# Attention values by pairs of heads in two column halves of the array, and every sixth unit's exponentials transposed on TensorE

## The chip, the core and the metric

The kernel runs on one core of one Trainium2 chip. The metric is the device time of one execution in microseconds (us). Five engines work side by side and meet at semaphores: TensorE (PE in the rows, its weight loads PEld), VectorE (DVE), ScalarE (ACT), GpSimd (POOL) and SyncE (SP), which issues the DMAs.

## The reference

Two layers of a backbone over 1024 latent tokens and 256 context tokens of width 1024, batch 1. Each layer normalises, projects once into three groups of heads (softmax attention, a bidirectional mLSTM, a pooling mixer), joins the three, projects out, adds to the stream, and then runs a SwiGLU block. The change touches the attention group alone, with 8 query heads of 64 over 2 key and value heads:

```python
s = jnp.einsum('bqhgd,bkhd->bhgqk', qi, k, preferred_element_type=F32) * scale
p = jax.nn.softmax(s, -1).astype(v.dtype)
return jnp.einsum('bhgqk,bkhd->bqhgd', p, v)
```

Latent queries see all 1280 tokens. Context queries see the 256 context tokens, and only in the first layer; the second layer has none.

## The kernel before

Each layer first makes all projections with eight free PSUM banks, and then goes over to a phase "s", in which six banks are two score buffers of three banks (`bank3`, tile `Sp`) and two banks are left for everything else (`bank`, tag `bk`). Operands of most matmuls are split into a high and a low float16 half, and a product is three matmuls (`TERMS`: high by high, high by low, low by high).

The attention loop runs over units. A unit is one head of one block of 128 latent queries; there are 64 in a layer, and layer 0 has four more, each of four heads of one block of context queries. Iteration i of the loop does, in the order of the program:

* `front` of unit i: scores into `Sp` (L1311, six matmuls for 1280 keys), their maximum by DVE (L1315), a small DVE step (L1320), and the exponentials by ACT into `pf` in float32, with their sum into `sums`;
* `split` of unit i-1: the high half `phl` by ACT (by DVE for every eighth unit, L1334), the low half by POOL (L169), and one DMA transpose of both halves into `pT` (L1340, on the queue of SP). There are two buffers of `pf`, three of `phl` and five of `pT`;
* the fill: a step of the output projection (`wout`, L1371, twelve matmuls into a bank `pwo`, which DVE adds to `X`), paced by a budget per iteration;
* `back` of unit i-5: the values. Each 128x128 block of `pT` is the stationary operand, and the 64 columns of V stream past it (L1353), thirty matmuls for a head, into one bank `pv` that is held for all eight heads of a query block.

After the eighth head `att_finish` divides by the sums (`ao`), splits into `aoh` (ACT and DVE) and transposes by DMA into `mixT` (L1365), the operand of the output projection. The framework that builds the kernel lists each engine's instructions by priority and readiness, so that the order on an engine is near the order of the program, but not the same.

Other lines that are used as prices: L919 writes two column halves of a bank with 64-wide stationary operands in the mLSTM part; L618 transposes float32 blocks by TensorE at the end; L471 and L1946 are projections.

Of the kernel before, what the change touches and what calls it, by code (L numbers as in the profile page):

```python
# [9 lines left out]
F32 = mybir.dt.float32  # L10
F16 = mybir.dt.float16
# [7 lines left out]
P = 128  # L19
# [62 lines left out]
def hybrid_kernel(ctx: ExitStack, tc: tile.TileContext, I, out, dbg=None):  # L82
    nc = tc.nc
    V, S, G, TE, DMA = nc.vector, nc.scalar, nc.gpsimd, nc.tensor, nc.sync
    MUL, ADD, SUB, MAX, MIN = ALU.mult, ALU.add, ALU.subtract, ALU.max, ALU.min
# [10 lines left out]
    PFB, PHB, PTB = 2, 3, 5  # L96
# [21 lines left out]
    def bank(name="bk"):  # L118
        return cur["b"].tile([P, 512], F32, tag="bk", name=name)
# [8 lines left out]
    def pt_(shape, dt, tag, bufs=1, name=None):  # L128
        return cur["w"].tile(list(shape), dt, tag=tag, name=name or tag, bufs=bufs)

    def f2k(shape=(P, 512), dt=F32, name="f2k"):
        return pt_(shape, dt, "f2k", F2K[cur["kind"]], name)


    mm = TE.matmul
# [6 lines left out]
    def preload():  # L142

        p = S.preload_act_table_set("natural_log_exp_and_others").ins
        for j in tabs["last"]:
            after(p, j)
        tabs.update(pre=p, last=[], kind="el")

    def act(o, i, f=AF.Copy, **kw):
        if f in (AF.Exp, AF.Ln) and tabs["kind"] != "el":  # L150
            preload()
        b = S.activation(o, i, f, **kw).ins  # L152
        if f in (AF.Exp, AF.Ln):
            after(b, tabs["pre"])
            tabs["last"] = tabs["last"][-7:] + [b]
        elif f in (AF.Tanh, AF.Silu):
            if tabs["kind"] != f:
                for j in tabs["last"]:
                    after(b, j)
                tabs.update(last=[], kind=f)  # L160
            for j in tabs["last"][-1:]:
                after(b, j)
            tabs["last"] = [b]
# [4 lines left out]
    def tt(o, a, b, op, e=None):  # L168
        (e or V).tensor_tensor(o, a, b, op=op)  # L169
# [23 lines left out]
    def pump(n=1):  # L193
        for _ in range(n):
            for g in list(threads):
                try:
                    next(g)
                except StopIteration:
                    threads.remove(g)
# [18 lines left out]
    idn = con.tile([P, P], F32, name="idn")  # L218
# [36 lines left out]
    pv = bank("pv")  # L255
# [203 lines left out]
    TERMS = ((0, 0), (0, 1), (1, 0))  # L459
# [272 lines left out]
    pv = bank("pv")  # L732
# [5 lines left out]
    pv = None  # L738
    nx = {}

    for l in range(DEPTH):
        last = l == DEPTH - 1
        h1 = mixT = h2 = T1
        qkv = actb = T2
# [462 lines left out]
        for (t0, n) in BLOCKS:  # L1207
            if t0 in nx:
                drain(nx.pop(t0))
            for r in range(3):  # L1210
                if t0 >= T and last and r == 2:
                    continue
                if l == 0 and t0 < T:
                    pb = pf0[r][t0 // 512]
                else:
                    pb = bank("pfm")
                    fm(pb[:, :n], wf[r], h1, t0, n)
                held.append((r, t0, n, pb))
                pb = None
# [3 lines left out]
            while held and t0 > 0:  # L1223
                r_, t_, n_, pb = held.pop(0)
                fst[r_](t_, n_, pb[:, :n_])
                pb = None
                pump()
        w = w_get(("in", l, O_MG))
        pb = bank("pmg")
# [66 lines left out]

        class Unit:
            def __init__(self, i, qt, hs, qs):
                self.i, self.qt, self.hs, self.qs = i, qt, hs, qs
                self.nk, self.k0 = (NTOK, 0) if qt < 8 else (TC, T)  # L1300
                self.n = self.nk * len(hs)

# [25 lines left out]
                        accum_out=self.qs[1][:, h:h + 1])  # L1328

            def split(self):  # L1330
                i, n, pf = self.i, self.n, self.pf
                hl = pt_((P, 2, NTOK), F16, "phl", PHB)
                if i % 8 == 0:
                    V.tensor_copy(hl[:, 0, :n], pf[:, :n])  # L1334
                else:
                    act(hl[:, 0, :n], pf[:, :n])
                tt(hl[:, 1, :n], pf[:, :n], hl[:, 0, :n], SUB, G)
                self.pT = pt_((P, 2, 10, P), F16, "pT", PTB)
                if n == NTOK:
                    DMA.dma_start_transpose(out=self.pT.rearrange("p a k c -> p (a k) c"), in_=hl.rearrange("p a t -> p (a t)"))  # L1340
                else:
                    for a in range(2):
                        DMA.dma_start_transpose(out=self.pT[:, a, :n // P], in_=hl[:, a, :n])

            def back(self):
                if self.hs[0] == 0:
                    self.qs[0] = bank("pv")
                nkt = self.nk // P
                for e, h in enumerate(self.hs):
                    kv = h // 4  # L1350
                    for kt in range(nkt):
                        for j, (a, b) in enumerate(TERMS):
                            mm(self.qs[0][:, h * 64:h * 64 + 64], self.pT[:, a, e * nkt + kt],  # L1353
                               qkv[:, 6, b, self.k0 + kt * P:self.k0 + (kt + 1) * P][:, kv * 64:kv * 64 + 64],
                               start=(kt == 0 and j == 0), stop=(kt == nkt - 1 and j == 2))

        def att_finish(qt, pv_, sums):
            V.reciprocal(sums, sums)
            o = f2k((P, 8, 64), F32, "ao")
            tt(o, pv_.rearrange("p (h e) -> p h e", h=8), sums.unsqueeze(2).to_broadcast([P, 8, 64]), MUL)  # L1360
            oh = f2k((P, 4, 2, P), F16, "aoh")
            ov = o.rearrange("p (k x) e -> p k (x e)", x=2)
            act(oh[:, :, 0], ov)
            tt(oh[:, :, 1], ov, oh[:, :, 0], SUB)
            DMA.dma_start_transpose(out=mixT[:, 0:4, :, qt * P:(qt + 1) * P].rearrange("p k a t -> p (k a) t"),  # L1365
                                    in_=oh.rearrange("p k a c -> p (k a c)"))

        def wout(w, k0, m, t0, n, pb):
            for k in range(4):
# [48 lines left out]
        units = []  # L1418
        for qt in range(8):
            qs = [None, pt_((P, 8), F32, "sums", 3)]  # L1420
            units += [Unit(len(units) + h, qt, [h], qs) for h in range(8)]
            if qt < 2 and not last:
                qs = [None, pt_((P, 8), F32, "sums", 3)]
                units += [Unit(len(units) + g, 8 + qt, list(range(4 * g, 4 * g + 4)), qs) for g in range(2)]
        done = [-1]
        nt = {}
        fill = fills()
        nu = len(units)
        budget = 0.0
        fill_ffn = first_ffn()  # L1430

# [4 lines left out]
        for i in range(nu + 5):  # L1436
            now[0] = i
            if i < nu:
                units[i].front()
            if 1 <= i <= nu:  # L1440
                units[i - 1].split()
            if i >= 3:
                budget = min(budget + pace(i / nu), 3.0)
                if budget > 0:
                    c = next(fill, None)
                    if c is None:
                        c = next(fill_ffn, 0)
                    budget -= c
            if i >= 5:
                u = units[i - 5]  # L1450
                u.back()
                if u.hs[-1] == 7:
                    att_finish(u.qt, *u.qs)
                    if u.qt < 8:
                        done[0] = u.qt
                units[i - 5] = u = None
            pump()
        for _ in fill:
            pass
        units = fill = None  # L1460
# [133 lines left out]
        raws, sums, rawuse, made, live_s = {}, {}, {}, {}, [0]  # L1594
# [344 lines left out]
        for bi, (t0, n) in enumerate([(0, 512), (512, 256), (768, 256)] if last else blks):  # L1939
            sums = None if last else Sums(t0, n)  # L1940
            for m in range(NK):
                w = piece("last", m)
                pb = bank("pdn")
# [8 lines left out]
            if bi == 0:  # L1952
# [3 lines left out]
                pb = None  # L1956
# [7 lines left out]
            if bi == 0 and not last:  # L1964
                sums = rms_sum(t0, n)
# [5 lines left out]
            sums = None  # L1971
# [33 lines left out]
```

## Time and profile before

| | us |
|---|---|
| median of three runs | 2797.26 (2795.92 to 2797.89) |
| the profiled execution | 2801.78 |
| its span, first to last instruction | 2800.0 |
| PE busy in the span | 2562.9 (92%) |
| DVE busy | 1883.6 (67%) |
| ACT busy | 1387.2 (50%) |
| POOL busy | 1288.5 (46%) |

A busy time is the time covered by at least one instruction of the engine. Matmuls are pipelined, so that each is shown longer than the distance from one start to the next; distances of starts are read from groups of them. The DMA share is the mean over 16 DMA engines and may go over 1 where packets overlap.

### The profile page before, as it was taken

How to read it: one execution, taken by the hardware profiler on the slowest of the kernel's cores; microseconds unless marked ns; L12 is line 12 of the kernel's file. 1: busy time of each engine (PE TensorE's matmuls, PEld its weight loads, DVE VectorE, ACT ScalarE, POOL GpSimd, SP SyncE). 2: the span in 40 equal slices, each digit the busy share in tenths (PEclk: the TensorE clock that was granted, in tenths of full speed). 3: DMA queues.
4: the chain of work that ended last, by engine and by line, in shares of the span. 5: the costliest groups of instructions: out<-in, count | busy, mean ns of one | idle time of the engine just before them, and what ended most of it. 6: DMA issues, size and time to landing. Idle time of an engine off the chain costs nothing. (4 is left out here: it accounts for less than half of the span.)

```text
span 2800.0 us, 53595 instructions
## 1 busy us (share of the span) xinstructions
PE 2562.9 (92%) x21331; PEld 1496.8 (53%) x21331; DVE 1883.6 (67%) x3217; ACT 1387.2 (50%) x2650; POOL 1288.5 (46%) x979
## 2 busy tenths in 40 slices
PE   7999988887799999999999998988878799999997
PEld 5875555555455555555555674545554344444444
DVE  5458867779856655656566557866677766576666
ACT  5345457776443434434344445466764444444353
POOL 1124446674434434344443213456764555555651
PEclk9999999999899999999999999999999999999999
DMA  9544499996222232322212222499993121211211
GB/s 298 143 122 115 126 208 187 195 186 129 61 83 84 83 88 80 89 84 83 68 39 78 69 61 64 124 183 188 195 188 80 45 61 53 61 53 53 61 53 76
DMA packets 650640, 300.95 MB, mean 107 GB/s; under 512 B 381896, under 2 KB 639764, under 8 KB 649876
## 3 DMA queue, kind: packets, MB, share of 16 engines
q1 hardware_dynamic: 650212, 297.45, 44.2%
q8 instruction: 167, 2.74, 0.4%
q14 instruction: 85, 0.70, 0.1%
q10 hardware_dynamic: 176, 0.07, 0.0%
HBM read 176.19 MB, written 20.87 MB: 70 GB/s over the span
## 5 line engine op out<-in xcount | busy, mean ns | idle before, releaser
L1900 PEld LDWEIGHTS <-hlp 128*128 128x128 f16 x5040 | 492.9, 98 | 610.1 <-issue 49.5
L1900 PE MATMUL Swb<-T,hlp 128*128 128x512 f16 x1920 | 446.4, 382 | 30.8 <-DVE sg L166 14.7
L169 POOL TENSOR_TENSOR phl<-pf,phl 128x1280 f16<-128x1280 f32 (+1 forms) x132 | 346.3, 2625 | 187.7 <-ACT phl L152 129.4
L166 DVE SCALAR_TENSOR_TENSOR hlp<-ws,hlp 128x512 f16<-128x512 f32 (+1 forms) x320 | 228.9, 722 | 150.6 <-ACT hlp L152 119.9
L152 ACT ACTIVATE hlp<-ws 128x512 f16<-128x512 f32 (+1 forms) x320 | 163.6, 518 | 220.1 <-PE Swb L1900 89.8
L152 ACT ACTIVATE pf<-Sp,mx,rq 128x1280 f32<-128x1280 f32 (+1 forms) x144 | 189.2, 1315 | 103.4 <-DVE mx L1320 89.1
L1315 DVE TENSOR_REDUCE mx<-Sp 128x1 f32<-128x1280 f32 (+1 forms) x132 | 194.9, 1477 | 64.5 <-PE Sp L1311 59.5
L1371 PE MATMUL pwo<-T,hl 128*128 128x512 f16 (+1 forms) x960 | 196.5, 356 | 38.0 <-DVE X L166 20.0
L1900 PE MATMUL Swc<-T,hlp 128*128 128x512 f16 x960 | 227.2, 379 | 0.0
L1311 PE MATMUL Sp<-T 128*128 128x512 f16 (+1 forms) x800 | 172.9, 355 | 58.5 <-ACT pf L152 56.1
L1900 PE MATMUL Swb<-tq,hlp 128*128 128x512 f16 x960 | 220.5, 379 | 2.5 <-ACT T L152 2.3
L466 PE MATMUL pfm<-T,hl 128*128 128x512 f16 (+1 forms) x1032 | 217.0, 364 | 4.2 <-ACT E L152 4.1
L152 ACT ACTIVATE T<-sg 128x512 f16<-128x512 f32 (+1 forms) x170 | 100.0, 600 | 229.4 <-POOL sg L169 154.8
L166 DVE SCALAR_TENSOR_TENSOR hlp<-st,hlp 128x256 f16<-128x256 f32 (+1 forms) x201 | 141.6, 709 | 89.8 <-ACT hlp L152 75.1
L169 POOL TENSOR_TENSOR ws<-st 128x256 f32<-128x256 f32 (+1 forms) x97 | 102.2, 1061 | 185.6 <-DMA st<-in_w_ffn_down_dram 83.3
L1912 PE MATMUL dx<-T,hlp 128*128 128x256 f16 x1440 | 177.9, 273 | 10.6 <-DVE hlp L166 6.4
L169 POOL TENSOR_TENSOR X<-X,T 128x512 f32<-128x512 f32 x80 | 113.2, 1415 | 147.4 <-DVE X L166 111.1
L1900 PE MATMUL Swa<-T,hlp 128*128 128x512 f16 x720 | 169.1, 380 | 0.0
L1912 PEld LDWEIGHTS <-hlp 128*128 128x128 f16 x1440 | 139.3, 100 | 43.0 <-issue 9.1
L1371 PEld LDWEIGHTS <-hl 128*128 128x128 f16 x960 | 98.0, 103 | 119.8 <-issue 53.3
L152 ACT ACTIVATE phl<-pf 128x1280 f16<-128x1280 f32 (+1 forms) x115 | 144.9, 1261 | 30.3 <-DMA pT<-phl 27.9
L152 ACT ACTIVATE hlp<-st 128x256 f16<-128x256 f32 (+1 forms) x201 | 101.2, 510 | 114.6 <-PE Swb L1900 73.2
(320 smaller groups left out, 4733.6 us busy)
## 6 DMA issues: line engine op xcount, KB each, us to landing
T<-in_w_ada_dram SPq DMA_DIRECT2D x48, 512.0 KB
rawa<-in_w_ada_dram SPq DMA_DIRECT2D x48, 512.0 KB
st<-in_w_in_dram SPq DMA_DIRECT2D x32, 512.0 KB
st<-in_w_out_dram SPq DMA_DIRECT2D x64, 256.0 KB
st<-in_w_ffn_gate_dram SPq DMA_DIRECT2D x32, 512.0 KB
st<-in_w_ffn_up_dram SPq DMA_DIRECT2D x30, 512.0 KB
st<-in_w_ffn_down_dram SPq DMA_DIRECT2D x30, 512.0 KB
xs<-X SPq DMA_DIRECT2D x4, 2048.0 KB
```

Source lines behind the costliest of these rows:

```text
L152: b = S.activation(o, i, f, **kw).ins
L166: V.scalar_tensor_tensor(o, a, s, b, op0=o0, op1=o1)
L169: (e or V).tensor_tensor(o, a, b, op=op)
L466: mm(o, w[:, a, k, :], h[:, k, b, t0:t0 + n], start=(k == 0 and j == 0), stop=(k == nk - 1 and j == 2))
L1311: mm(Sp[:, e * nk + b0:e * nk + b0 + m], ql, qkv[:, 4 + h // 4, a, k0 + b0:k0 + b0 + m], start=(a == 0), stop=(a == 1), skip_group_check=True)
L1315: r = V.tensor_reduce(mx[:, :ne], Sp[:, :n].rearrange("p (e k) -> p e k", e=ne), axis=AX.X, op=MAX)
L1371: mm(pb, w[:, a, k, :], mixT[:, k0 + k, b, t0:t0 + n], start=(k == 0 and j == 0), stop=(k == 3 and j == 2))
L1900: mm(o, w[:, a, k, :], B[:, b], start=(s in "172" and k == 0 and j == 0), stop=(k == kh(i) - 1 and j == 2), skip_group_check=True)
L1912: mm(dbank[i][:, r * 256:(r + 1) * 256], w[:, a, k, :], B[:, b], start=(first and k == 0 and j == 0), stop=(not first and k == kh(i) - 1 a ...
```

## The change

Units of one head are counted, and the 6th, 12th and so on (ten in each layer) are turned on TensorE: there is no `phl`, no POOL work and no DMA. The unit's ten 128x128 blocks of `pf` are transposed in float32 in groups of four, four and two into a bank `turn`; ACT writes the high half from it into `pT`, and DVE the low half. The three groups stand ahead of the fill, behind it, and behind the values.

The values are made for two heads at a time, every second iteration. Now V is the stationary operand, 64 columns wide, and 128 columns of `pT` stream; the even head writes partitions 0 to 63 of a bank and the odd head 64 to 127, in turn, so that the result comes out already transposed. The reciprocals of the two sums are spread over 64 partitions each by two float32 matmuls against the identity, copied out by ACT, multiplied in by DVE, and ACT and DVE write the two halves straight into `mixT`. The bank is held for one pair. `att_finish` and its DMA transpose go.

```diff
             def split(self):
                 i, n, pf = self.i, self.n, self.pf
+                if i in turned:
+                    self.pT = pt_((P, 2, 10, P), F16, "pT", PTB)
+                    self.parts = [self.turn(k, min(4, 10 - k)) for k in range(0, 10, 4)]
+                    return
...
-            def back(self):
-                if self.hs[0] == 0:
-                    self.qs[0] = bank("pv")
...
-                            mm(self.qs[0][:, h * 64:h * 64 + 64], self.pT[:, a, e * nkt + kt],
-                               qkv[:, 6, b, self.k0 + kt * P:self.k0 + (kt + 1) * P][:, kv * 64:kv * 64 + 64],
-                               start=(kt == 0 and j == 0), stop=(kt == nkt - 1 and j == 2))
-        def att_finish(qt, pv_, sums):
-            V.reciprocal(sums, sums)
-            o = f2k((P, 8, 64), F32, "ao")
-            tt(o, pv_.rearrange("p (h e) -> p h e", h=8), sums.unsqueeze(2).to_broadcast([P, 8, 64]), MUL)
-            oh = f2k((P, 4, 2, P), F16, "aoh")
...
-            act(oh[:, :, 0], ov)
-            tt(oh[:, :, 1], ov, oh[:, :, 0], SUB)
-            DMA.dma_start_transpose(out=mixT[:, 0:4, :, qt * P:(qt + 1) * P].rearrange("p k a t -> p (k a) t"),
-                                    in_=oh.rearrange("p k a c -> p (k a c)"))
+            def turn(self, k, m):
+                def go():
+                    tb = bank("turn")
+                    for c in range(m):
+                        TE.transpose(tb[:, c * P:(c + 1) * P], self.pf[:, (k + c) * P:(k + c + 1) * P], idn)
+                    tv = tb[:, :m * P].rearrange("p (k c) -> p k c", k=m)
+                    act(self.pT[:, 0, k:k + m], tv)
+                    tt(self.pT[:, 1, k:k + m], tv, self.pT[:, 0, k:k + m], SUB)
+                return go
+        def values(us, pair):
...
+            V.reciprocal(sums[:, hs[0]:hs[0] + 2], sums[:, hs[0]:hs[0] + 2])
+            pb = bank("pv")
+            for g, h in enumerate(hs):
+                mm(pb[64 * g:64 * g + 64, P:2 * P], sums[:, h:h + 1].to_broadcast([P, 64]), idn, start=True, stop=True)
+            u = f2k((P, 2, P), F32, "ao")
+            act(u[:, 0], pb[:, P:2 * P])
+            for kt in range(nkt):
+                for j, (a, b) in enumerate(TERMS):
+                    for g, h in enumerate(hs):
+                        un = us[g if len(us) == 2 else 0]
+                        mm(pb[64 * g:64 * g + 64, 0:P], qkv[:, 6, b, k0 + kt * P:k0 + (kt + 1) * P][:, kv * 64:kv * 64 + 64],
+                           un.pT[:, a, un.hs.index(h) * nkt + kt], start=(kt == 0 and j == 0), stop=(kt == nkt - 1 and j == 2),
+                           skip_group_check=True)
+            tt(u[:, 1], pb[:, 0:P], u[:, 0], MUL)
+            q = slice(qt * P, (qt + 1) * P)
+            act(mixT[:, pair, 0, q], u[:, 1])
+            tt(mixT[:, pair, 1, q], u[:, 1], mixT[:, pair, 0, q], SUB)
...
+        turned = [u.i for u in units if len(u.hs) == 1][5::6]
...
+            if parts:
+                parts.pop(0)()
             if i >= 3:
...
+            if parts:
+                parts.pop(0)()
             if i >= 5:
                 u = units[i - 5]
-                u.back()
-                if u.hs[-1] == 7:
-                    att_finish(u.qt, *u.qs)
-                    if u.qt < 8:
-                        done[0] = u.qt
+                if len(u.hs) > 1:
+                    for e in range(0, len(u.hs), 2):
+                        values([u], u.hs[e] // 2)
+                elif u.hs[0] % 2 == 0:
+                    values([u, units[i - 4]], u.hs[0] // 2)
+                if u.hs[-1] in (6, 7) and u.qt < 8:
+                    done[0] = u.qt
                 units[i - 5] = u = None
+            while parts:
+                parts.pop(0)()
```

## Rows read from the trace of the kernel before

**Rows 1.** Windows: stretch, length, busy PE, PEld, DVE, ACT, POOL, clock, DMA share.

```profile
374.00:656.00 282.00, 238.62 (x2845) 155.83 (x2844) 210.60 (x254) 198.91 (x274) 188.46 (x82) 0.94 1.07 194
1827.00:2091.00 264.00, 212.59 (x2564) 134.17 (x2562) 182.16 (x213) 182.71 (x228) 177.13 (x73) 0.95 1.05 190
...
450.00:500.00 50.00, 46.71 (x572) 30.30 (x570) 37.32 (x46) 36.77 (x49) 33.35 (x13) 0.97 1.12 188
```

**Rows 2.** The same windows for the fill's line L1371 alone.

```profile
374.00:656.00 282.00, 107.30 (x553) 56.23 (x554) 0.94 1.07 194
1827.00:2091.00 264.00, 82.31 (x360) 36.95 (x361) 0.95 1.05 190
```

**Rows 3.** Line L1315 in each stretch: count, ns min/median/max, first and last start.

```profile
L1315 DVE TENSOR_REDUCE mx<-Sp x68: 1215/1483/1494, 375.1 to 653.5; 128x1 f32<-128x1280 f32 x64, 128x4 f32<-128x1024 f32 x4
...
L1315 DVE TENSOR_REDUCE mx<-Sp x64: 1474/1483/1493, 1827.4 to 2089.3; 128x1 f32<-128x1280 f32 x64
```

**Rows 4.** Tiles pT and aoh: DMA transposes on the queue of SP.

```profile
L1340 SPq DMA_TRANSPOSE pT<-phl x128: 2977/3284/5487, 383.1 to 2098.1; - x128
...
L1365 SPq DMA_TRANSPOSE T<-aoh x18: 1231/1283/2072, 428.3 to 2111.0; - x18
```

**Rows 5.** Waits, 374 to 656 us: total us, times, longest.

```profile
ACT phl L152 <- DMA pT<-phl: 11.8, 11, 2.3
```

**Rows 6.** Waits, 1827 to 2091 us.

```profile
ACT phl L152 <- DMA pT<-phl: 16.1, 11, 3.2
```

**Rows 7.** Timeline, 564 to 574 us, the end of a query block.

```profile
567.28 0.68 DVE L169 TENSOR_TENSOR ao<-pv,sums 128x512 f32<-128x512 f32 x1
567.89 2.73 DVE L166 SCALAR_TENSOR_TENSOR hl<-st,hl 128x512 f16<-128x512 f32 x1
568.00 0.63 ACT L152 ACTIVATE aoh<-ao 128x512 f16<-128x512 f32 x1 [1.95 <-DVE ao L169]
...
570.53 1.48 DVE L1315 TENSOR_REDUCE mx<-Sp 128x1 f32<-128x1280 f32 x1
571.94 1.02 DVE L169 TENSOR_TENSOR aoh<-ao,aoh 128x512 f16<-128x512 f32 x1
...
573.53 1.03 PE L1371 MATMUL pwo<-T,hl 128*128 128x512 f16 x3 [3.39 <-DVE X L166]
```

**Rows 8.** Timeline of PE at several places (start, length, group); last, line L919's durations.

```profile
548.43 1.04 PE L1353 MATMUL pv<-T,pT 128*128 128x64 f16 x30
549.31 1.25 PE L1311 MATMUL Sp<-T 128*128 128x512 f16 x6
...
151.16 0.39 PE L919 MATMUL pu<-X,kh 128*64 128x65 f16 x12
151.48 2.74 PE L471 MATMUL ptm<-hl,T 128*128 128x128 f16 x46
...
2769.36 1.04 PE L618 MATMUL pout<-idn,X 128*128 128x128 f32 x8
2770.23 0.82 PE L1946 MATMUL pdn<-T,hlp 128*128 128x256 f16 x6
...
L919 PE MATMUL pu<-X,kh x432: 192/195/263, 142.8 to 1671.8; 128*64 128x65 f16 x144
```

**Rows 9.** Lines by form: busy us, mean ns, idle before and its releasers.

```profile
L169 POOL TENSOR_TENSOR phl<-pf,phl 128x1280 f16<-128x1280 f32 x128 | 337.8, 2641 | 183.7 <-ACT phl L152 126.0 <-DVE phl L1334 47.8 <-DMA pT<-phl 3.7
...
L152 ACT ACTIVATE phl<-pf 128x1280 f16<-128x1280 f32 x112 | 141.8, 1267 | 30.2 <-DMA pT<-phl 27.9 <-ACT pf L152 0.5
...
L152 ACT ACTIVATE X<-pf 128x512 f16<-128x512 f32 x6 | 3.4, 587 | 0.2
...
L166 DVE SCALAR_TENSOR_TENSOR X<-pf,X 128x512 f16<-128x512 f32 x6 | 3.8, 677 | 0.0
...
L152 ACT ACTIVATE sa<-pada 128x128 f32<-128x128 f32 x80 | 21.9, 273 | 4.6 <-PE pada L483 3.5
...
L169 DVE TENSOR_TENSOR num<-pxi,tmq 128x130 f32<-128x130 f32 x68 | 17.4, 284 | 7.8 <-PE pxi L998 7.5
```

More of the change, by code (lines that the diff above doesn't have):

```diff
@@ L1298, in __init__ @@
             def __init__(self, i, qt, hs, qs):
-                self.i, self.qt, self.hs, self.qs = i, qt, hs, qs
+                self.i, self.qt, self.hs, self.qs, self.parts = i, qt, hs, qs, []
                 self.nk, self.k0 = (NTOK, 0) if qt < 8 else (TC, T)
@@ L1343, in split @@
                         DMA.dma_start_transpose(out=self.pT[:, a, :n // P], in_=hl[:, a, :n])
-            def back(self):
-                if self.hs[0] == 0:
-                    self.qs[0] = bank("pv")
[L1348 to L1352, printed above, removed]
-                            mm(self.qs[0][:, h * 64:h * 64 + 64], self.pT[:, a, e * nkt + kt],
-                               qkv[:, 6, b, self.k0 + kt * P:self.k0 + (kt + 1) * P][:, kv * 64:kv * 64 + 64],
-                               start=(kt == 0 and j == 0), stop=(kt == nkt - 1 and j == 2))
@@ L1357, in att_finish @@
-        def att_finish(qt, pv_, sums):
-            V.reciprocal(sums, sums)
-            o = f2k((P, 8, 64), F32, "ao")
-            tt(o, pv_.rearrange("p (h e) -> p h e", h=8), sums.unsqueeze(2).to_broadcast([P, 8, 64]), MUL)
-            oh = f2k((P, 4, 2, P), F16, "aoh")
-            ov = o.rearrange("p (k x) e -> p k (x e)", x=2)
-            act(oh[:, :, 0], ov)
-            tt(oh[:, :, 1], ov, oh[:, :, 0], SUB)
-            DMA.dma_start_transpose(out=mixT[:, 0:4, :, qt * P:(qt + 1) * P].rearrange("p k a t -> p (k a) t"),
-                                    in_=oh.rearrange("p k a c -> p (k a c)"))
+            def turn(self, k, m):
[7 more added lines that the diff above has]
+                return go
@@ new lines, in values @@
+        def values(us, pair):
+            qt, sums = us[0].qt, us[0].qs[1]
+            nkt, k0 = us[0].nk // P, us[0].k0
+            hs = (2 * pair, 2 * pair + 1)
+            kv = pair // 2
+            V.reciprocal(sums[:, hs[0]:hs[0] + 2], sums[:, hs[0]:hs[0] + 2])
[15 more added lines that the diff above has]
+            tt(mixT[:, pair, 1, q], u[:, 1], mixT[:, pair, 0, q], SUB)
@@ L1439, in hybrid_kernel @@
                 units[i].front()
+            parts = []
             if 1 <= i <= nu:
                 units[i - 1].split()
+                parts = units[i - 1].parts
+            if parts:
+                parts.pop(0)()
             if i >= 3:
```

## The prediction

> **What bounds the kernel now.** The change lives in the attention loops, so the first view to read is the table of windows, over the first layer's loop (374 to 656 us, called A) and the second's (1827 to 2091 us, B) [rows 1]. Together they are 546 us of the 2800, and nothing outside is touched but the ends of the loops. The reader is to see two things in it. PE is busy for 238.6 of 282 us and 212.6 of 264 us, a share of 0.826 over both; DVE 0.75 and 0.69, ACT 0.71 and 0.69, POOL 0.67. And the DMA share is 1.07 and 1.05: the DMA engines are full through both loops.
>
> Second, the fill's windows and the starts of the units [rows 2, 3]. A carries 107 us of output projection and B only 82 us, yet units begin every (653.5 - 375.1) / 67 = 4.16 us in A and every (2089.3 - 1827.4) / 63 = 4.16 us in B. What is the same per unit in both is the DMA transpose: 3.28 us on SP's queue, with 1.28 us more for each query block [rows 4], and between them the weights. So I read the transposes as the pace of B, where PE has slack, and as one of two paces in A. The waits agree as far as they go: ACT waits 11.8 us in A and 16.1 us in B for a `phl` buffer that a transpose has not yet read [rows 5, 6].
>
> Third, the timeline at the end of a query block, for what the DMA queue does not explain [rows 7]. `ao`, a weight split of 2.73 us and `aoh` stand on DVE around the maximum of a new unit, which starts only at 570.53, and PE then has sat idle for 3.39 us before its fill, for a bank that DVE gives back. This comes at the end of each of the 18 query blocks, larger or smaller. PE itself can run denser: in the stretch from 450 to 500 us it is busy for 46.71 of 50 us, 0.934 [rows 1].
>
> **The change part by part.**
>
> *Taken from DMA, SP and POOL.* Twenty transposes of 3.284 us and all 18 of 1.283 us [rows 4]: 65.7 + 23.1 = 88.8 us of SP's queue, 45.7 in A (10 units, 10 blocks) and 43.1 in B (10 units, 8 blocks). On SP the weight loads stand behind them and come earlier. POOL loses 20 x 2.641 = 52.8 us [rows 9]. The full DMA queue then has 236 us of work for A and 221 for B, and stops being the bound if the loops stay above that.
>
> *Values, on PE.* Before, thirty matmuls take from 548.43 to the next group at 549.31 [rows 8]: 0.88 us a head, 1.76 a pair. After, a pair has 30 steps of two half matmuls with 128 columns. The nearest rows are two. Full-width matmuls of 128 columns follow each other, 46 in 2.74 us, of which some 0.2 us is the last one's own tail: 0.056 us each. And at L919 two column halves with 64-wide weights have twelve matmuls of 65 columns in 0.39 us; less the last one's own 0.195 us, eleven distances in 0.195 us, 18 ns each, where one after the other the 65 columns alone would need 27 ns at 2.4 GHz, the granted clock being near 1 in the loops [rows 1, 8]. So halves run side by side, and I price a step at the 0.056 us of one matmul: 30 x 0.056 = 1.68 us. The bound above is two matmuls one after the other, 3.36 us.
>
> The array must also change between whole width and halves. After L919 the next whole-width group starts at 151.48, 0.32 us after its first start and so 0.125 us after its last, against distances of some 0.03 inside: 0.095 us for a change [rows 8]. The Trainium skill, TensorEngine Tiling (Array Packing), Key Properties, says that changing the mode drains the engine; the trace agrees, with these 0.095 us. There are two changes a pair, 0.19 us. The float32 matmuls that spread the reciprocals are bounded by the float32 blocks of L618, 8 from 2769.36 to 2770.23, 0.109 us each: 0.11 side by side, 0.22 otherwise, and I take 0.15 [rows 8]. A pair is then 1.68 + 0.19 + 0.15 = 2.02 against 1.76, +0.26 us; a pair of context heads, with 6 steps in place of 12 matmuls, 0.34 + 0.34 - 0.35 = +0.33. A has 32 and 8 of them: +10.9 us. B has 32: +8.3.
>
> *Turned units, on PE.* Ten float32 blocks of 0.109 us are 1.09 us a unit, +10.9 us in each loop. In all PE gets +21.8 in A and +19.2 in B: 260.4 and 231.8 us of work, 492.2 together.
>
> *ACT.* A pair gets two copies of 128x128 at 0.273; a block loses the 0.63 of `aoh` [rows 7, 9]; a turned unit has two and a half copies of 512 at 0.587 in place of 1.267. A: 21.8 - 6.3 + 2.0 = +17.5; B: 17.5 - 5.0 + 2.0 = +14.5. ACT comes to 216 and 197 us.
>
> *DVE.* A pair gets the product (0.284), the low half (a quarter of `aoh`'s 1.02, or 0.284) and a reciprocal, which I bound by 0.284 too: at most 0.85. A block loses 0.68 + 1.02. A turned unit gets two and a half low halves of 512 from PSUM at 0.677, 1.69 [rows 7, 9]. A: 34.0 - 17.0 + 16.9 = +34; B: 27.2 - 13.6 + 16.9 = +30. DVE comes to 245 and 213 us, still below PE. But DVE now has the second largest load, and it is DVE that gives back banks.
>
> *Banks.* Before, `pv` keeps one of the two small banks for a whole block, so that the fill has one. After, a pair keeps one for one pair, but 72 pairs and 60 groups of transposes take banks too. I cost this at nothing in the forecast, since the 3.39 us of [rows 7] is the kind of wait that gets shorter with a second bank; the other end is a rival.
>
> *What is behind the new waits.* The four transposes ahead of the fill wait for the exponentials of the unit before; behind them on PE stand the fill and the values. ACT's copy of the reciprocals waits for PE, and behind it are exponentials. The third group stands behind the values, and `pf` (two buffers) is kept till then. The end of each loop loses one DMA transpose ahead of the last quarter of the projection, but the last pair's matmuls come later by a head; I set this at nothing.
>
> **The sum.** With DMA no longer full, the largest load is PE's 492.2 us over the two loops. The forecast takes the densest share that PE shows now, 0.934: 260.4 / 0.934 = 278.8 and 231.8 / 0.934 = 248.2, against 282 and 264, so -3.2 and -15.8, together -19.0 us. That is above the 236 and 221 that the DMA queue needs. The profiled execution has 2801.78; less 19.0 it is 2782.8. The median of the runs is 0.99839 of that execution, so the forecast is 2778 us.
>
> **The rivals.** The same sum at another share of PE gives all but one of them; the time is unchanged at 492.2 / 546 = 0.901.
>
> *The banks and DVE take the place of the queue (slower).* 132 new holders of two banks wait for ACT and DVE to empty them, DVE with 64 us more to do. PE idles for 94.8 us in the loops now; the time grows once more than 53.8 us of idle is left or made new. At a share of 0.86 the loops take 572 us, +26, 2823; at today's 0.826 they take 596, +50, 2847. For it: PE waits for DVE in [rows 7], and DVE's load of 0.88 of A. Against it: the burst on DVE at each block's end is cut in four, and POOL, which works beside it, has 53 us less.
>
> *Nothing to see.* The wait moves from the queue to PE: a share of 0.89 to 0.91, 2792 to 2803.
>
> *Denser than ever seen.* The queue was behind nearly every wait, and PE goes over 0.96. The limit is PE without a gap, -53.8 us, 2743.
>
> *The halves do not run side by side with 128 columns (slower).* A step is then two matmuls, 0.112: +1.68 us for each of 64 pairs, +108 us on the loads of PE, 2880 or more. Against it are the 18 ns of L919 [rows 8]. The Trainium skill, TensorEngine Tiling (Array Packing), Restrictions, says that column tiling does without the fast weight load, and TensorE: Matmul & The Clock Gate, LDWEIGHTS, gives columns / 1.2 in ns, an estimate of 53 ns for 64 columns; two such loads one behind the other would be 107 ns a step, the same rival. The trace speaks against it: at L919 a load comes with every one of the matmuls that start 18 ns apart.
>
> **How the numbers follow.** Chances: forecast (share 0.91 to 0.96, 2764 to 2791) 0.48; denser (2743 to 2764) 0.10; nothing 0.11; banks and DVE 0.27; halves 0.04. A change of 0.2%, 5.6 us, is about what a measurement of this kernel can tell from none. Faster by more: 0.48 + 0.10 = 0.58. Within: 0.11. Slower: 0.27 + 0.04 = 0.31. The range for 8 times in 10 takes in most of the denser case and the banks' case up to a share of 0.86: 2748 to 2825. The forecast's own range is 2764 to 2791.
>
> **What the profile of the changed kernel would show.** DMA share under 1 in both loops, and no ACT wait for `pT`; if it is still full, the reading of the pace was wrong. Pairs of halves some 0.056 us apart; if 0.11, the halves do not overlap. B shorter by some 16 us and A by a few; if both shrink alike, the queue paced A too. PE's share above 0.9 in the loops; below that, its idle time will have DVE's or ACT's names on `turn`, `pv` and `pwo`, and the prediction fails there.

## The result and the profile after

The changed kernel takes 2889.6 us (median of four runs, 2884.1 to 2893.6) against 2797.6 for the kernel before: a ratio of 1.0328, 95% interval [1.0307, 1.0349]. The forecast of 2778 and its range up to 2825 are missed, and the sign is wrong. The profiled execution of the changed kernel took 2884.12 us, with a span of 2882.4. In the experiments below, "measured" gives the median in us, its ratio to the kernel before, run again beside it, and the 95% interval of the ratio. The kernel before had medians from 2797.6 to 2801.6 in these series, so that differences between runs of different series are uncertain by some 4 us. Executions some hundreds of us longer at a lower granted clock, one in each of two series, are left out.

The first view is the windows of the two loops in the changed kernel, with the columns of [rows 1], and under it line L1315, the maximum that starts each unit, as in [rows 3].

```profile
374.00:700.00 326.00, 272.09 (x3013) 165.89 (x3014) 233.87 (x362) 208.52 (x355) 161.14 (x71) 0.94 0.71 139
1878.00:2168.00 290.00, 237.06 (x2633) 139.64 (x2632) 216.40 (x305) 187.96 (x291) 145.17 (x60) 0.95 0.76 141
```

```profile
L1315 DVE TENSOR_REDUCE mx<-Sp x68: 1202/1481/1493, 376.0 to 697.1; 128x1 f32<-128x1280 f32 x64, 128x4 f32<-128x1024 f32 x4
...
L1315 DVE TENSOR_REDUCE mx<-Sp x64: 1469/1478/1493, 1878.8 to 2165.5; 128x1 f32<-128x1280 f32 x64
```

From the first unit to the last, A takes 321.1 us where it took 278.4, and B 286.7 where it took 261.9. That is +67. Most of the rest is behind the loops: from the start of the last maximum to the end of the last matmul of the values it was 16.8 and 16.2 us, and is 25.8 and 27.7, which is +20. The profiled executions differ by 82 us, as the part behind the second layer's values is 5 us shorter (694 before, 689 after). The DMA share fell to 0.71 and 0.76, as the forecast wanted, and yet no time came of it: PE is busy for 509.15 of 616 us, a share of 0.827, as before (0.826). The DMA transposes of `pT` are 108 in place of 128, and somewhat shorter than in [rows 4]:

```profile
L1345 SPq DMA_TRANSPOSE pT<-phl x108: 2986/3116/5654, 383.8 to 2182.5; - x108
```

ACT's wait for a `phl` buffer [rows 5, 6] is gone from A. These stand there now (waits, 374 to 700 us: total us, times, longest):

```profile
ACT T L152 <- DVE ao L169: 22.8, 15, 3.1
DVE ao L169 <- PE pv L1376: 20.5, 15, 2.3
...
DVE sums L1366 <- ACT pf L152: 18.4, 15, 1.7
...
ACT ao L152 <- PE pv L1369: 13.9, 10, 4.9
...
PE pv L1376 <- ACT ao L152: 8.7, 9, 2.1
DVE T L169 <- ACT T L152: 8.1, 10, 1.8
```

All six belong to the new chain of a pair: reciprocal (DVE, L1366), its spread (PE, L1369), a copy (ACT, `ao`), the matmuls (PE, L1376), the product (DVE, `ao`), the high half (ACT, `T`) and the low half (DVE, `T<-ao,T`). The chain crosses between engines six times. The last link has the shortest wait in this list, 8.1 us, and is the dearest all the same. Its durations (min/median/max), and a stretch of the timeline:

```profile
L169 DVE TENSOR_TENSOR T<-ao,T x72: 274/293/2660, 399.0 to 2198.8; 128x128 f16<-128x128 f32 x72
```

```profile
426.36 1.47 DVE L1315 TENSOR_REDUCE mx<-Sp 128x1 f32<-128x1280 f32 x1
...
427.68 2.61 POOL L169 TENSOR_TENSOR phl<-pf,phl 128x1280 f16<-128x1280 f32 x1 [4.83 <-ACT phl L152]
427.77 2.66 DVE L169 TENSOR_TENSOR T<-ao,T 128x128 f16<-128x128 f32 x1
...
430.36 0.20 DVE L1320 TENSOR_SCALAR mx<-mx,rq 128x1 f32<-128x1 f32 x1
430.48 1.47 DVE L1315 TENSOR_REDUCE mx<-Sp 128x1 f32<-128x1280 f32 x1
430.66 1.42 ACT L152 ACTIVATE pf<-Sp,mx,rq 128x1280 f32<-128x1280 f32 x1 [2.21 <-DVE mx L1320]
```

The reader is to see that one subtraction of 128x128 takes 2.66 us, nearly ten times its shortest. It starts 0.09 us after POOL's subtraction and ends 0.14 us after it (430.43 against 430.29). A stall inside an instruction is shown as busy time, so no list of waits names it; what shows it is the distance between median and maximum. It is no single case: 35 of the 72 start while an instruction of POOL runs, take 1.66 us in the mean and all end behind it, 32 of them by 0.145 to 0.151 us; the other 37 take 0.274 to 0.293. Behind it on DVE stand the scaling of the maximum (L1320), for which the exponentials on ACT then wait 2.21 us, and the next unit's maximum.

The last view is the timeline of one pair's matmuls:

```profile
548.01 0.44 PE L1369 MATMUL pv<-idn,sums 128*64 128x128 f32 x4
...
548.38 1.25 PE L1311 MATMUL Sp<-T 128*128 128x512 f16 x6
...
551.24 0.27 ACT L152 ACTIVATE ao<-pv 128x128 f32<-128x128 f32 x1
...
551.55 1.87 PE L1376 MATMUL pv<-pT,T 128*64 128x128 f16 x60 [0.35 <-ACT ao L152]
```

Sixty half matmuls in 1.87 us are 0.056 us for a pair of halves and some 0.2 of tail: the halves run side by side, at the price that was forecast. But the spread stands 3.5 us ahead of them, with whole-width matmuls between, and the sixty wait for ACT's copy out of their own bank.

The clock column of the windows asks for a second look at PE's busy time. Another pair waits 1.95 us for the same copy, and the clock then stands at its lower level, 1.2 in place of 2.4 GHz (timeline, and the window of these 3.3 us):

```profile
591.01 3.36 PE L1376 MATMUL pv<-pT,T 128*64 128x128 f16 x60 [1.95 <-ACT ao L152]
```

```profile
591.10:594.40 3.30, 3.30 (x61) 3.13 (x61) 1.18 (x1) 0.68 (x2) 2.17 (x2) 0.50 0.37 73
```

The same sixty matmuls take 3.36 us in place of 1.87, so that busy time grows here without more work. What makes the clock fall at one place and not at another was not tried. A mean of 0.94 is 12% of the time at the lower level; from the means I estimate 68 us there in the 616 us of the loops, against 60 us of 546 before.

### The profile page after: what moved, and what is told of

It reads as the page before. It is cut to its first block, busy times and chain, and to the rows that moved or that the text cites. A ratio compares the mean times of both kernels' runs of the same rounds, so it can differ in the third digit from the quotient of the medians.

```text
span 2882.4 us, 54835 instructions
## 1 busy us (share of the span) xinstructions
PE 2631.7 (91%) x21819; PEld 1521.2 (53%) x21819; DVE 1951.8 (68%) x3439; ACT 1412.3 (49%) x2816; POOL 1234.7 (43%) x959
## 5 line engine op out<-in xcount | busy, mean ns | idle before, releaser
L169 POOL TENSOR_TENSOR phl<-pf,phl 128x1280 f16<-128x1280 f32 (+1 forms) x112 | 292.4, 2613 | 313.7 <-ACT phl L152 209.7
L1311 PE MATMUL Sp<-T 128*128 128x512 f16 (+1 forms) x800 | 182.0, 355 | 44.1 <-ACT pf L152 42.1
L1315 DVE TENSOR_REDUCE mx<-Sp 128x1 f32<-128x1280 f32 (+1 forms) x132 | 194.5, 1474 | 33.1 <-PE Sp L1311 32.5
L466 PEld LDWEIGHTS <-hl 128*128 128x128 f16 x1032 | 100.8, 102 | 97.9 <-issue 21.6
L1387 PEld LDWEIGHTS <-hl 128*128 128x128 f16 x960 | 95.2, 101 | 108.4 <-issue 42.3
```

What stands on the lines that cost most here:

```text
L466: mm(o, w[:, a, k, :], h[:, k, b, t0:t0 + n], start=(k == 0 and j == 0), stop=(k == nk - 1 and j == 2))
L1311: mm(Sp[:, e * nk + b0:e * nk + b0 + m], ql, qkv[:, 4 + h // 4, a, k0 + b0:k0 + b0 + m], start=(a == 0), stop=(a == 1), skip_group_check=True)
L1315: r = V.tensor_reduce(mx[:, :ne], Sp[:, :n].rearrange("p (e k) -> p e k", e=ne), axis=AX.X, op=MAX)
L1387: mm(pb, w[:, a, k, :], mixT[:, k0 + k, b, t0:t0 + n], start=(k == 0 and j == 0), stop=(k == 3 and j == 2))
```

## The experiments

### One part of the change alone

```diff
-        turned = [u.i for u in units if len(u.hs) == 1][5::6]
+        turned = []
```

> The changed kernel with no turned unit: all exponentials go by DMA again, the values stay by pairs. Theory P (the pairs cost: four mode changes and a wait of PE for ACT's copy of the reciprocals in each pair): most of the 92 us stays, 2850 to 2880 us. Theory T (the turned units cost: PE waits for fresh exponentials and for banks): the loss is gone, 2795 to 2820 us. If the DMA queue paced the loops before, its load is back here and the time is not below 2797 in either case.

Measured: 2870.1, 1.0243 [1.0226, 1.0259]. The pairs alone carry about 70 of the 90 us.

The other half is the kernel before with `turned`, `turn` and the calls of the parts put in, and `back` and `att_finish` kept:

> The kernel before with every sixth unit turned on TensorE; values, division and their DMA transpose as before. Theory P: 22 us of transposes on PE and a few waits, less what the DMA queue gives back: 2790 to 2825 us. Theory T: most of the loss, 2850 to 2885 us.

Measured: 2833.5, 1.0113 [1.0098, 1.0128], so +32. Beside the pairs they add 2889.6 - 2870.1 = 19.5, or 24 with each run's own kernel before, which is less, though not clear of the intervals. Neither part gains anything.

### Is the DMA queue the pace?

This is the kernel before, in which only the high halves are transposed by DMA. The values read the high half where they read the low half, so that every engine has as much work as before and the queue about half; the result is another one.

```diff
-  DMA.dma_start_transpose(out=self.pT.rearrange("p a k c -> p (a k) c"), in_=hl.rearrange("p a t -> p (a t)"))
+  DMA.dma_start_transpose(out=self.pT[:, 0], in_=hl[:, 0])
...
-  mm(self.qs[0][:, h * 64:h * 64 + 64], self.pT[:, a, e * nkt + kt],
+  mm(self.qs[0][:, h * 64:h * 64 + 64], self.pT[:, 0, e * nkt + kt],
```

> The kernel before, but only the high halves of the exponentials are transposed by DMA; the values read the high half in place of the low half too, so the output differs. All engines do the same work, the queue half of it. If the DMA queue paced the loops (the prediction's reading): they shrink to PE's densest share, 2745 to 2775 us. If the ring of scores, maximum and exponentials and the order on PE and DVE pace them: 2787 to 2800 us.

Measured: 2773.4, 0.9901 [0.9885, 0.9918]. Its windows:

```profile
374.00:643.00 269.00, 232.03 (x2834) 153.91 (x2834) 210.08 (x254) 199.12 (x275) 188.14 (x82) 0.96 0.63 125
1814.00:2063.00 249.00, 206.15 (x2564) 130.88 (x2563) 181.73 (x212) 183.10 (x229) 178.18 (x73) 0.97 0.64 122
```

With 40% of the DMA load gone and nothing added on any engine, the loops give back 28 us, and PE stops at 438.18 of 518, a share of 0.846. A takes 265.1 us from its first maximum to its last and B 247.1, so both shrink alike, by 13 and 15. The queue is one pace of both loops, but the next one lies 5% below it: with the queue relieved and no work added, PE stays far from the 0.934 of the forecast.

### The spread's place on PE

```diff
-            for g, h in enumerate(hs):
-                mm(pb[64 * g:64 * g + 64, P:2 * P], sums[:, h:h + 1].to_broadcast([P, 64]), idn, start=True, stop=True)
-            u = f2k((P, 2, P), F32, "ao")
-            act(u[:, 0], pb[:, P:2 * P])
             for kt in range(nkt):
...
+            for g, h in enumerate(hs):
+                mm(pb[64 * g:64 * g + 64, P:2 * P], sums[:, h:h + 1].to_broadcast([P, 64]), idn, start=True, stop=True)
+            u = f2k((P, 2, P), F32, "ao")
+            act(u[:, 0], pb[:, P:2 * P])
             tt(u[:, 1], pb[:, 0:P], u[:, 0], MUL)
```

> The changed kernel with the two matmuls that spread the reciprocals, and ACT's copy of them, behind the pair's values in place of ahead of them. The same work in another order: PE no longer waits for ACT before the values, and the array changes mode twice a pair in place of nearly four times. Theory P: some 20 us of waits and 14 us of mode changes go, 2845 to 2862 us. Theory T: within 10 us of 2890.

Measured: 2875.3, 1.0264 [1.0248, 1.0279]. That is 14 us (18 against each run's own kernel before), about half of the least that was expected. The theory that the order on PE is the loss falls as the main one.

### The low half beside POOL

```diff
-            tt(mixT[:, pair, 1, q], u[:, 1], mixT[:, pair, 0, q], SUB)
+            tt(mixT[:, pair, 1, q], u[:, 1], mixT[:, pair, 0, q], SUB, G)
```

> The changed kernel with one edit: the subtraction that makes the low half of a pair's values (T<-ao,T, 72 of them, 68.6 us on DVE in the changed kernel, 0.27 us when POOL is idle and up to 2.66 us when it starts beside POOL's long subtraction) moves from DVE to POOL. Theory H (held): DVE's instruction is held until POOL's ends, and the next unit's maximum stands behind it; with the low half on POOL, 68.6 - 72 x 0.27 = 49 us of DVE's time go, most of it from the time: 2835 to 2865. Theory S (a pair's reciprocal on DVE waits for the newest exponentials) expects the waits of the reciprocals for pf to stay, and little change, 2875 to 2895. The theory that PE's mode changes and the order on PE cost the time expects 2880 to 2895.

Measured: 2845.9, 1.0159 [1.0143, 1.0175], so -44. On POOL the same 72 instructions take 0.52 us each (lines by form, busy us and mean ns), as they now stand in POOL's own queue:

```profile
L169 POOL TENSOR_TENSOR T<-ao,T 128x128 f16<-128x128 f32 x72 | 37.4, 521 | 50.2 <-ACT T L152 47.5 <-PE ms L556 2.7
```

One operand `G` is half of the loss. The theory of the held instruction stands, at about the size of its excess on DVE (49 us). What the run does not part is that the other 20 us of this work leave DVE too, and that the granted clock rises from 0.94 and 0.95 to 0.97 in both loops (374 to 683 us and 1855 to 2128).

### The reciprocals' wait

```diff
-            qs = [None, pt_((P, 8), F32, "sums", 3)]
+            qs = [None, [pt_((P, 2), F32, "sums", 12) for _ in range(4)]]
...
-                        accum_out=self.qs[1][:, h:h + 1])
+                        accum_out=self.qs[1][h // 2][:, h % 2:h % 2 + 1])
```

> The changed kernel with one edit: each pair of heads has its own tile of sums (two columns) in place of two columns of the block's tile of eight, so that a pair's reciprocal depends on the exponentials of its own two heads alone. Theory S: for two of four pairs the reciprocal waited for the exponentials just issued, of another head with columns in the same tile, and the next maximum stood behind it on DVE; 29 such waits with 30 us of idle DVE go, and the time falls by about that: 2850 to 2870. Theory H (held low halves): no change, 2880 to 2895. The rival that a wait of an engine with 29% of idle time costs nothing: no change too.

Measured: 2891.6, 1.0318 [1.0299, 1.0336]: no change, and the wait itself stayed (idle us before the line, and what ended it):

```profile
L1366 DVE RECIPROCAL sums<-sums 128x2 f32<-128x2 f32 x72 | 11.5, 160 | 30.9 <-ACT pf L152 30.7
```

So the shared tile was not its reason. In the trace a reciprocal that waits starts when its own second head's exponentials end, often right behind that head's maximum: the wait comes from its early place on DVE. The next edit moves it:

```diff
-            V.reciprocal(sums[:, hs[0]:hs[0] + 2], sums[:, hs[0]:hs[0] + 2])
+            after(V.reciprocal(sums[:, hs[0]:hs[0] + 2], sums[:, hs[0]:hs[0] + 2]).ins, tabs["mx"])
```

> The changed kernel with one edit: a pair's reciprocal is ordered on DVE behind the scaling of the maximum of the step's newest unit (L1320), where it stood up to four units earlier, right behind the maximum of its own second head, whose exponentials it then had to wait for with the next maximum behind it (29 waits, 30 us of idle DVE). Theory S2, in place of the tile of sums, which the run before refuted: the order on DVE makes the wait; without it 10 to 30 us go, 2860 to 2880. Rival: DVE's idle time there costs nothing, as it does not bound the loop: 2885 to 2895.

Measured: 2942.9, 1.0518 [1.0500, 1.0536], 53 us worse: both theories missed. Its waits from 374 to 700 us:

```profile
ACT pf L152 <- DVE sums L1366: 61.0, 21, 5.3
DVE ao L169 <- PE pv L1376: 49.4, 20, 4.8
PE pv L1369 <- DVE sums L1366: 39.0, 21, 3.5
```

A late reciprocal makes PE wait with the spread, and the exponentials wait for it too. That fits the tile of eight sums into which later heads of the block still write: with own tiles and a late reciprocal (below, with other edits besides) the same wait is 9.4 us. What the idle DVE ahead of an early reciprocal costs does not come out of this run; the chain behind a late one costs more.

### The pairs, mended

The pairs alone, with low half on POOL, spread behind the matmuls, and own sums:

> The pairs alone (no turned units; 2870.1 with nothing mended), with three edits: low half on POOL, own sums for each pair, and the spread of the reciprocals with its ACT copy moved behind the pair's matmuls. If theories H and S and the order on PE are the whole of the loss, the pairs then cost only their 0.26 us on PE and bring the freed queue: 2785 to 2805. If the pairs lose by something else (bank turnover, mode changes, the ends of the loops), it stays above 2820.

Measured: 2799.9 against 2800.3 for the kernel before on the same chip, 0.9996 [0.9986, 1.0005]. All 70 us are gone, and nothing is gained. Then the late reciprocal on top of it:

> The pairs mended (low half on POOL, spread behind the values, own sums: 2799.9) with the same edit of the reciprocal's place on DVE. There the reciprocals wait 78.5 us in 51 waits for the exponentials. Theory S2: a third to two thirds of it comes off the time: 2750 to 2780. Rival (idle time that costs nothing, or the wait moves to the maximum that waits for PE anyway): 2793 to 2803.

Measured: 2801.2, 1.0003 [0.9991, 1.0015]: no change. The reciprocals' wait is gone, as the lines of the two runs show, the first without and the second with the late reciprocal:

```profile
L1366 DVE RECIPROCAL sums<-sums 128x2 f32<-128x2 f32 x72 | 11.7, 163 | 78.5 <-ACT pf L152 78.5
```

```profile
L1366 DVE RECIPROCAL sums<-sums 128x2 f32<-128x2 f32 x72 | 10.6, 153 | 0.8 <-ACT pf L152 0.8
```

But the spread's lines of the same two runs show what came in its place:

```profile
L1376 PE MATMUL pv<-idn,sums 128*64 128x128 f32 x288 | 29.5, 280 | 0.0
```

```profile
L1376 PE MATMUL pv<-idn,sums 128*64 128x128 f32 x288 | 30.4, 290 | 25.9 <-DVE sums L1366 25.6
```

78 us of DVE's waiting went, and 26 us of PE's, for the late reciprocals, came. The time fits the rival, a wait that cost nothing, and fits as well a wait that was worth what the new one costs. No run parts the two.

### How the two edits share the loss

> The whole change with two of the edits that were run alone: low half on POOL (alone -44 us) and the spread of the reciprocals behind the pair's matmuls (alone -14). If the two losses are separate, they add: 2889.6 - 44 - 14 = 2831, taken 2825 to 2838. If they hide each other (with DVE held, the wait of the matmuls for ACT's copy of the reciprocals did not count, and comes out once DVE is free), the two together give more than their sum: 2795 to 2820. If they are one loss seen twice: 2840 to 2848.

> The pairs alone (2870.1) with the low half on POOL as the only edit. If the held low half is the same loss here as in the whole change: 2870 - 44 = 2826, taken 2818 to 2834, and the rest down to 2800 is the place of the spread. If the low half is the whole of the pairs' loss: 2800 to 2810. If the place of the spread is most of it: 2840 or more.

Measured: 2822.5, 1.0079 [1.0064, 1.0094], and 2824.2, 2824.3 and 2835.6 in three executions, 1.0108 [1.0081, 1.0135]. For the whole change the four corners are, in us:

| | spread ahead | spread behind |
|---|---|---|
| low half on DVE | 2889.6 | 2875.3 |
| low half on POOL | 2845.9 | 2822.5 |

The edits give 44 and 14 alone and 67 together, 9 us more than their sum. Against each run's own kernel before (1.0328, 1.0264, 1.0159 and 1.0079) it is 4 or 5 us, and with intervals of some 0.002 either way on each ratio it stays open whether the two losses add or hide each other a little. For the pairs alone the steps are 2870.1, then 2824 to 2836 with the low half on POOL, then 2799.9 with the spread behind (and own sums, which were not parted from it there). The windows of the whole change with both edits (the last maxima start at 670.0 and 2101.4 us), and of the pairs mended:

```profile
374.00:672.00 298.00, 259.21 (x3124) 165.64 (x3123) 213.84 (x332) 211.21 (x359) 182.39 (x110) 0.97 0.82 155
1846.00:2103.00 257.00, 220.47 (x2644) 134.23 (x2643) 185.57 (x275) 187.14 (x290) 159.05 (x88) 0.99 0.84 158
```

```profile
374.00:657.00 283.00, 248.47 (x3024) 157.58 (x3023) 196.95 (x302) 208.21 (x338) 206.57 (x119) 0.96 0.99 186
1829.00:2087.00 258.00, 216.86 (x2677) 131.88 (x2676) 176.02 (x253) 189.11 (x278) 190.00 (x100) 0.97 1.03 186
```

PE's share is 479.68 / 555 = 0.864 in the one and 465.33 / 541 = 0.860 in the other. The clock has risen from 0.94 and 0.95 to 0.97 and 0.99 with both edits: by the same estimate as above 23 us at the lower level in place of 68. PE does half the work in such time, so that up to some 22 of the 67 us can have come back by way of the clock.

### The turned units' place

This is the kernel before with the turned units alone (2833.5 above), with all three groups moved behind the values:

```diff
-            if parts:
-                parts.pop(0)()
             if i >= 3:
...
-            if parts:
-                parts.pop(0)()
             if i >= 5:
...
             while parts:
                 parts.pop(0)()
```

> The kernel with the turned units alone (values as before the change), with all three groups of transposes issued after the fill and the values of the step in place of one before, one between and one behind. Theory W: the turned units cost 32 us because PE stands at the first group and waits for the exponentials (44.9 us in 24 waits), with fill and values behind it; at the end of the step the exponentials are there, and the time is 2795 to 2815. Rival: it is PE's added work, 20 x 1.09 us and its share of idle time, and ACT's and DVE's copies: 2828 to 2838, as before the edit.

Measured: 2816.5, 1.0055 [1.0039, 1.0070]. Between the two: 17 of the 32 us were the place, 16 remain. The lines of the transposes, before and after this edit:

```profile
L1353 PE MATMUL turn<-idn,pf 128*128 128x128 f32 x200 | 36.8, 302 | 34.2 <-ACT pf L152 20.7 <-DVE pT L169 8.6 <-DVE mx L1320 2.1
```

```profile
L1353 PE MATMUL turn<-idn,pf 128*128 128x128 f32 x200 | 34.9, 292 | 23.6 <-DVE pT L169 12.1 <-ACT pf L152 5.2 <-DVE X L166 4.6
```

PE waited 20.7 us for the exponentials, and then 5.2, which is near what the time gave back. The 44.9 us of the expectation count the waits of these matmuls and of their weight loads (24.2) together, and the two overlap.

> The whole change, turned units too, with all edits: low half on POOL, spread behind the values, own sums, late reciprocal, and the three groups of transposes of a turned unit at the end of its step. If the turned units at the end of the step cost what they cost alone there (16 us), 2765 to 2800; if with the queue relieved by both parts they pay, below 2765; if PE is the bound by then, 21.8 us of work over a share of 0.85 more than the pairs mended: 25 us above that run.

Measured: 2823.6, 1.0089 [1.0072, 1.0106], 22 above the pairs mended with the late reciprocal. The lines of the transposes, first with groups ahead of the fill and low half and spread mended (2822.5), then in this run:

```profile
L1354 PE MATMUL turn<-idn,pf 128*128 128x128 f32 x200 | 33.2, 287 | 28.4 <-ACT pf L152 21.2 <-DVE ao L169 4.7 <-DVE pT L169 2.4
```

```profile
L1354 PE MATMUL turn<-idn,pf 128*128 128x128 f32 x200 | 32.8, 283 | 9.7 <-DVE ao L169 4.4 <-ACT pf L152 1.9 <-DVE pT L169 1.7
```

PE's wait for the exponentials fell from 21.2 to 1.9 us, and the time is the same (2822.5 and 2823.6). But this run has the late reciprocal too, and the spread on PE, which did not wait in the first of the two, waits for it:

```profile
L1376 PE MATMUL pv<-idn,sums 128*64 128x128 f32 x288 | 30.2, 290 | 26.7 <-DVE sums L1366 26.5
```

So 19 us of one wait of PE went and 26 us of another came. The turned units at the end of the step beside mended pairs, without the late reciprocal, were not run. The turned units cost 22.6 us beside mended pairs in the first of these runs (which has no own sums) and 22.4 in the second, about the 20 x 1.09 = 21.8 us of transposes that they put on PE.

### The same held subtraction in the kernel before

```diff
-            tt(oh[:, :, 1], ov, oh[:, :, 0], SUB)
+            tt(oh[:, :, 1], ov, oh[:, :, 0], SUB, G)
```

> The kernel before with one edit: the block's low half (aoh<-ao,aoh, 18 of 128x512, 23.8 us on DVE; 10 start beside POOL's long subtraction and take 1836 ns in the mean, the 8 others 682) moves from DVE to POOL. Theory H: 23.8 us of DVE go, 11.5 of them of being held, and the maximum behind them comes earlier: 2780 to 2795. Rival: the block's end is not on the path in the kernel before, or POOL's load takes its place: 2796 to 2804.

Measured: 2796.6, 0.9989 [0.9979, 0.9998]. Of 23.8 us taken off DVE some 4 came through, less than what can be told from nothing: held or not, at a block's end this work hardly counts for the time. Beside the run with half the DMA load, which leaves work out, none beats the kernel before by more.

## Why the prediction was wrong

**The low half on DVE** ("at most 0.85 a pair") is the step that failed first, and it was a term of the sum that was mis-sized. It was priced at 0.26 or 0.284; it took 68.4 us over 72, 0.95 each, and moving it, with its 49 us of excess, gave 44 of time. In the sum it stood in DVE's load alone, which was taken to bound nothing; what it did was to hold up the next unit's maximum and, behind it, exponentials and scores. The row that should have warned was ahead of the prediction: in [rows 7] `aoh` takes 1.02 where `ao`, of the same size, takes 0.68; I took a quarter of the 1.02 and did not ask why it was longer. Products that read `pv` or `turn` from PSUM show no such spread (`pT<-turn,pT` of 128x512 has a median of 0.68 as its price said). The Trainium skill, SBUF — State Buffer, Summary: rules for kernel authors, says that where DVE has two SBUF inputs while a GpSimd instruction reads SBUF, the second to issue blocks until the first finishes. The trace agrees: 2.66 us, ending 0.14 us behind POOL's. The change had moved a subtraction from 18 large ones at blocks' ends to 72 small ones among the units, each able to take 2.6 us when held, with a maximum behind it.

**The values' order** was costed by durations (0.15 for the spread, two changes of width) with no wait. The spread stood 3.5 us apart from its matmuls, which then waited for ACT. Behind the matmuls it costs 14 us less, and 23 with the low half on POOL, a difference that the intervals do not clear. This is half of the rival "the banks and DVE take the place of the queue". Whether the wait for ACT costs the time, or the bank that a pair then holds 3.5 us longer, was not parted. A small slip beside it: the change of width was read as 0.125 less 0.03, where the 18 ns of the same rows make it 0.107, which adds 1.7 us to the sum.

**The share of PE** (0.934, "the densest share that PE shows now") is the step that would have failed even so. With both edits PE's share is 0.864, near the rival at 0.86. That this rival gave 2823 and that run took 2822.5 is in part luck: the rival has 572 us for the loops where they take 555, and the ends, which it leaves alone, are 10 us longer. A dense stretch of 50 us is a place where PE has work at hand; it is not what a loop reaches when one wait is taken out. The run with half the DMA load found 0.846 with no work added.

**The queue** was read rightly as full and wrongly as the one pace of B: some 40% off its load is worth 28 us, in A as much as in B, and then something else paces both. The 23 us of the queue's work freed by mended pairs, against some 19 us more on PE, are worth zero; the twenty turned units free 66 us more and cost their PE time in full.

**The ends of the loops** ("I set this at nothing") took 20 us in the changed kernel; with low half and spread mended the tails are 17.2 and 25.4 us, so 10 of it went. With all edits they are 16.8 and 17.1, as before the change, but the loops are longer by as much.

**Right** were the 0.056 us of a pair of halves, the fall of the DMA share and of ACT's wait, and PE's load, once the low half and the spread are mended: from the start of each loop's window to the end of its last values PE is busy for 508.6 us against 471.5 before, +37 where the sum has +41. In the changed kernel the same work takes 543.7 us, with more of it at the lower clock, which the sum left out. The mark set beforehand, that with PE's share below 0.9 the waits would name `pv` and `turn`, came true in part: the longest wait of PE's matmuls in A is for `Sp`, 19.3 us, as it was before (19.5). The rival that decides was named with a chance of 0.27, but ended at 2847 for an unchanged share: short by 43 us, as PE was busy for 509 us in place of 492 (17 / 0.827 = 20 us), and the ends took another 20.

**Open** is what keeps PE at 0.86 when queue, held subtractions and the spread's place are out of the way. Two waits that looked like it were taken out, DVE's for the reciprocals (78 us) and PE's for the turned units' exponentials (19 of 21 us), but each time the late reciprocal put a wait of 26 us on PE, so that neither is ruled out. For the same reason it is not settled what the turned units' place, worth 17 us in the kernel before, is worth beside mended pairs. How much of the loss came by way of the clock was not parted from the waits either.

## What to carry to other kernels

When a small operation is multiplied and moved among long ones of another engine, price it by the longest row of its kind, not by its median, and look at what stands behind it on its engine. When a full resource is relieved, take the next limit from a run that relieves it and adds nothing, not from the densest stretch of the trace. And when a wait is taken out and the time stays, read the new waits before calling the old one free: here two waits went, and a new one of PE's came each time. The costliest stall of all stood in no list, being counted as busy.

## What the runs showed of the hardware

A 128x128 subtraction on DVE with both inputs in SBUF takes 274 ns, and up to 2660 when it starts beside POOL's 2.6 us subtraction; it ends some 0.15 us after POOL's does. With one input in PSUM (`ao<-pv,ao`) the same size takes 262 to 293 ns, beside POOL or not. Of the same kind as the first are `aoh` in the kernel before (682 ns in the mean, 1836 when it starts beside POOL).

Two column halves of the array with 64-wide weights and 128 columns each sustain 0.056 us for the pair of them over thirty steps, weight loads included, the same as one whole-width matmul of 128 columns; that is at a granted clock of 1.00, and at 0.50 the sixty take 3.36 us in place of 1.87.
